# The gate and up products of both feed-forward layers: plain products over 512 tokens in place of Strassen's seven

## The chip, the cores and the metric

The kernel runs on one core of one Trainium2 chip. The metric is device time in microseconds (us) of one execution. Before the change it is 1904.37 us, the median of 3 runs (1902.75 to 1905.04). A TensorE instruction is called a product here: a stationary operand of 128x128 is loaded, and a moving operand of 256 or 512 columns is streamed through it into PSUM.

## The reference

Two layers act on 512 latent tokens and 256 context tokens, with 1024 features. Layer 0 mixes the tokens with a gated recurrence, layer 1 with windowed attention; each ends in a feed-forward part. Every half is wrapped in a norm that is scaled and shifted by vectors `ml`, `mc`, which come from products with `ada_w`. Only the latent tokens are returned. The part that the change touches is the first product of `swiglu`, `u @ w_in`, for the latent tokens of both layers:

```python
def swiglu(u, w_in, w_out):
    gt, up = jnp.split(u @ w_in, 2, axis=-1)
    return (jax.nn.silu(gt) * up) @ w_out
...
        x_lat = x_lat + ml[2] * rms_norm(y_lat, ng[1])
        h_lat = swiglu(modulate(x_lat, ng[2], ml[3], ml[4]), ffn_w_in[l], ffn_w_out[l])
        x_lat = x_lat + ml[5] * rms_norm(h_lat, ng[3])
```

`w_in` has 1024 rows and 2 x 2816 columns: 22 tiles of 128 gate features and 22 of up features.

## The kernel before

Activations lie feature-major: 8 tiles of 128 features x 512 tokens. Each fp32 operand is split into a high part (rounded to `fp32r`) and the rest, a low part, so that a product becomes three: high x high, low x high, high x low. The function `acc3` (line 180 issues it) does the three for each chunk of 128 contraction features. A weight tile of 128x1024 is loaded by SyncE (`raw`), cast on ScalarE or GpSimd (`whi`), and VectorE subtracts (`wlo`); `wload` does this for plain products (lines 130 to 133). There are four `raw`, three `whi` and three `wlo` buffers. `engines(ph)` names the engine of each stage's casts by a letter (`a` ScalarE, `p` GpSimd, `d` VectorE).

For the latent tokens a **unit** is one gate tile and one up tile. `ffn_in_s` does a unit by Strassen's method. `str_weights` loads the two tiles, forms sums and differences of quarters (lines 502 to 515, mostly on GpSimd, one on VectorE) and splits the seven results (`split`, lines 483 and 486). `str_unit` does seven products on quarters: 7 x 4 chunks x 3 = 84 products of 256 columns. It then combines the results on VectorE and ScalarE, and GpSimd multiplies by the gate (line 553). The moving operands `Uh`, `Ul`, and the sums of them that Strassen's products need, are made by `str_operand` (lines 568, 574 and 585 on VectorE), one half of the tokens after the other.

The rest of the program is written as generators. `merge(main, side, ratio)` gives the side `ratio` steps for each step of the main line, and a scheduler then orders all engines' instructions from that text, by priorities and a simulated timeline. Tiles of [128, 512] come from 63 slots, which a plan hands out by lifetimes; the `ar` tiles take such slots too. SyncE issues all transfers in one queue, in order.

The stages that matter, in order:
- "co": the context's output products (`ffn_out`), with the latent residual and `str_operand` beside them (`lat_mid`).
- Layer 0's feed-forward (`lat_ffn0`): 13 units, then the output products over these 13 hidden tiles (`out_part`), then 9 units. Beside it (`merge`, ratio 0.7) runs the context's residual and `ada_gen`, which makes layer 1's modulation vectors. `ada_gen` takes 80 tiles `ar` of 256 KB from memory and multiplies each (line 251) with a stationary operand of 32 columns, on one quarter of the array's columns: tile k goes to quarter k % 4. A Strassen unit is 8 steps of `merge`'s main line.
- "lo": the rest of the output products, and layer 1's norm of the context, which needs these vectors.
- Layer 1: attention, its output products ("wo", with 16 more `ar` tiles), and "f1": the first 5 units as plain products, 256 tokens at a time (`ffn_in_c`), the second half's residual and operands beside them. Then 8 Strassen units, output products, 9 Strassen units, and the last output products.

Of the kernel before, what the change touches and what calls it, by code (L numbers as in the profile page):

```python
# [45 lines left out]
def block_kernel(ctx, tc, plan, xT, cT, vecs, w2, cst, atm, rope, ada, rec_a, rec_v, rec_g, rec_o, qk_w, v_w, wo_w, ff_in, ff_out, out):  # L46
# [124 lines left out]
    def acc3(ps_, wparts, act):  # L171
        """three products a chunk; cfg["ll"]: those with the low part of the moving operand last."""
# [9 lines left out]
    def gemm_b(ps, whalves, ahi, alo, st, tt):  # L182
        """ps [128 tok, 256] = act[:, tok]^T w; whalves: (hi, lo) pieces of KD / len k x 256 columns."""
# [10 lines left out]
    # ---- PSUM: one bank per tile  # L194
# [13 lines left out]
    def follow(key, ins):  # L208
        """issue `ins` behind the last one of its lane on the same engine."""
# [8 lines left out]
    def psg():  # L218
        """accumulator of a dense product."""
# [4 lines left out]
    # ---- adaLN vectors, feature-major  # L224
# [45 lines left out]
    def scale_vec(a, g, plus_one, o=None, hfs=(0, 1)):  # L270
        """(1 + a) * g or a * g, both streams."""
# [9 lines left out]
    # ---- norms (feature-major)  # L281
    class Acc:
        """sums of squares over features, in two running parts [128, r, nt]; adds alternate
        between GpSimd and DVE where `dve` is set."""
# [9 lines left out]
        def add(self, src, sl, sv=None, own=False):  # L294
            """own: a tile of its own for these squares, which spares the addition."""
# [24 lines left out]
    def rstd_bc(acc, sl):  # L320
        """1 / rms of every token in sl, on all partitions (PSUM)."""
# [22 lines left out]
    def preload_sqrt():  # L344
        """brings the square root's table in behind what ACT has been given so far."""
# [12 lines left out]
    def norm_mod(tiles, acc, G, sh, j, u, sl, st=None):  # L358
        """u (hi, lo) = norm(x) * G + sh (acc None: tiles are normalised)."""
# [40 lines left out]
    def residual(tiles, ys, yacc, gg, j, xacc, sl, pat=""):  # L400
        """x += gate * norm(y); xacc collects the new x's squares."""
# [26 lines left out]
    def evac_y(st, m, p_, ys, yacc, sl):  # L428
        """projection output tile m: copy and squares."""
# [7 lines left out]
    def proj_out(st, src, nparts, a, ys, yacc, ms, sl):  # L437
        """feature-major output tiles ms of 128 features: src(m, part) -> (ap, n)."""
# [35 lines left out]
    # ---- Strassen's products for a dense layer on the latent tokens: two output tiles of features,  # L474
    # two halves of the contraction, two halves of the tokens.
    SCH = (("s2", "11", 0, 0), ("s5", "22", 0, 1), ("A22", "c", 1, 0), ("A11", "b", 1, 1), ("s1", "a", 3, 0), ("s7", "e", 2, 0),
           ("s6", "d", 2, 1))

    def split(src, w):
        hi = wp.tile([P, 1024], F32R, name=uid("whi"), tag="whi", bufs=WB)  # L480
        lo = wp.tile([P, 1024], F32R, name=uid("wlo"), tag="wlo", bufs=WB)
        if 'a' == "a":
            nc.scalar.copy(hi[:, :w], src)  # L483
        else:
            nc.gpsimd.tensor_scalar(hi[:, :w], src, 1.0, 0.0, ALU.mult, ALU.add)
        nc.vector.tensor_sub(lo[:, :w], src, hi[:, :w].bitcast(F32))  # L486
        return hi, lo

    def str_weights(src1, src2, w):
        """the seven stationary operands of [A11 | A12], [A21 | A22], w columns a quarter."""  # L490
        with tc.high_priority(offset=200):
            raw = []
            for s_ in (src1, src2):
                r = wp.tile([P, 1024], F32, name=uid("raw"), tag="raw", bufs=WB + 1)
                nc.sync.dma_start(out=r[:, : 2 * w], in_=s_)
                raw.append(r)
            g, u_ = raw
            L, R, B = slice(0, w), slice(w, 2 * w), slice(0, 2 * w)
            ws = hpool["p"].tile([P, 1024], F32, name=uid("ws"), tag="ws", bufs=WS)
            e = {"p": nc.gpsimd, "d": nc.vector}  # L500
            en = [e[c] for c in "pppdp"]
            en[0].tensor_sub(ws[:, R], u_[:, L], g[:, L])
            en[1].tensor_add(u_[:, L], u_[:, L], u_[:, R])
            en[2].tensor_add(ws[:, L], g[:, L], g[:, R])
            W = {}

            def put(hl, *names):
                for i, n_ in enumerate(names):
                    W[n_] = tuple(t[:, i * w : (i + 1) * w] for t in hl)

            put(split(u_[:, B], 2 * w), "s2", "A22")
            put(split(ws[:, B], 2 * w), "s5", "s6")
            en[3].tensor_sub(g[:, R], g[:, R], u_[:, R])  # L513
            put(split(g[:, B], 2 * w), "A11", "s7")
            en[4].tensor_add(g[:, L], g[:, L], u_[:, R])  # L515
            put(split(g[:, L], w), "s1")
        return W

    def str_unit(W, B, nk):
        """[C21 | C12] and [C11 | C22] in SBUF."""  # L520
        T = [None] * 4
        o = ut([P, 2, 256], name="so")
        x = ut([P, 2, 256], name="sx")
        y = ut([P, 2, 256], name="sy")
        for w, b, t, c in SCH:
            if T[t] is None:
                T[t] = ps("mm" if t == 3 else "kv").rearrange("p (c n) -> p c n", c=2)
            acc3(T[t][:, c, :], [W[w] + (nk,)], B[b])
            yield
            with tc.high_priority(offset=cfg["evp"]):  # L530
                if w == "s5":
                    nc.scalar.copy(y, T[0])
                elif w == "A11":
                    nc.vector.tensor_add(o, T[1], y)  # L534
                    for i in range(2):
                        nc.vector.tensor_sub(x[:, i, :], T[1][:, i, :], y[:, 1 - i, :])
                elif w == "s1":
                    m1 = ut([P, 256], name="m1")
                    nc.scalar.copy(m1, T[3][:, 0, :])
                elif w == "s6":  # L540
                    nc.vector.tensor_add(y, T[2], m1.unsqueeze(1).to_broadcast([P, 2, 256]))
        (nc.gpsimd if "p" == "p" else nc.vector).tensor_add(y, y, x)  # L542
        return o, y

    def ffn_in_s(l, U, h, ms, m0=0):
        for m in ms:
            W = str_weights(ff_in[l, m, 0], ff_in[l, m, 1], 512)
            o, y = yield from str_unit(W, U, 4)
            nc.scalar.activation(o[:, 1, :], o[:, 1, :], AF.Silu)
            nc.scalar.activation(y[:, 0, :], y[:, 0, :], AF.Silu)  # L550
            f = ut([P, 2, 256], name="fs")
            for i in range(2):
                (nc.gpsimd if "pp"[i] == "p" else nc.vector).tensor_mul(f[:, i, :], y[:, i, :], o[:, i, :])  # L553
            hh = h[0][m - m0]
            f = f.rearrange("p c n -> p (c n)").unsqueeze(1)
            nc.scalar.copy(hh, f)
            nc.vector.tensor_sub(h[1][m - m0], f, hh.bitcast(F32))
            yield

    def str_operand(tiles, xacc, G, sh, j, U, conv):  # L560
        """generators (one per token half) of the moving operands of u = norm(x) * G + sh; conv: also
        the plain parts of each half, for products without Strassen's sums."""
        F = [[None] * 4, [None] * 4]

# [12 lines left out]
        def half(hf):  # L577
# [21 lines left out]
            if hf == 0:  # L599
                return  # L600
# [1275 lines left out]
```

## Time and profile before

| what | value |
|---|---|
| median of 3 runs | 1904.37 us (1902.75 to 1905.04) |
| the profiled execution's own span | 1901.0 us |
| VectorE busy | 1277.6 us (67%) |
| ScalarE busy | 824.9 us (43%) |
| GpSimd busy | 875.7 us (46%) |
| mean granted TensorE clock | 0.969 |
| mean transfer rate | 121 GB/s |

The profile is of one execution; its times run from the start of its span. PE is TensorE, PEld its weight loads, DVE VectorE, ACT ScalarE, POOL GpSimd, SP SyncE. A name such as `ps_kv<-Uh,wlo` is output and inputs of an instruction, and L180 is the line that issued it. Products overlap in the pipeline, so the duration of one (0.28 us for 256 columns) says less than the step from one's start to the next one's.

### The profile page before, as it was taken

To read this page: it belongs to the slowest core of one execution; us is meant where nothing else is said; L and a number is where in the kernel's file an instruction comes from. 1 tells how busy PE (TensorE), PEld (TensorE's weight loads), DVE (VectorE), ACT (ScalarE), POOL (GpSimd) and SP (SyncE) were. 2 spreads that over 40 slices of the span, in tenths; PEclk is the share of its full clock that TensorE was granted. 3 is DMA by queue.
4 is the path that set the end of the run, shared out by engine and by line. 5 is a ranking of instruction groups with operands and counts; after the bars stand their busy time and mean duration, and the time that the engine had idled before them with its cause. 6 is when DMAs were issued, how large, how long until landed. Compare 5 with 4: busy or idle time off the path is not lost. (4 is left out here: it accounts for less than half of the span.)

```text
span 1901.0 us, 31663 instructions
## 1 busy us (share of the span) xinstructions
PE 1774.9 (93%) x12467; PEld 1537.4 (81%) x12467; DVE 1277.6 (67%) x1846; ACT 824.9 (43%) x1503; POOL 875.7 (46%) x789
## 2 busy tenths in 40 slices
PE   6889999998999999899999989899999888999897
PEld 3878678797999989776888888786787888888886
DVE  4985445566667529976853887778755988726866
ACT  3643554234645546443522443435755434403431
POOL 3665303334120026665632674424444657725755
PEclk9989999999999999899999999899999999999999
DMA  9435556210334544575232224311013432332233
GB/s 330 136 100 185 171 178 216 68 51 33 116 130 145 183 135 142 200 259 198 82 108 81 89 80 132 101 47 56 13 56 122 135 101 77 103 99 77 89 87 118
DMA packets 84005, 229.45 MB, mean 121 GB/s; under 512 B 9328, under 2 KB 14192, under 8 KB 83856
## 3 DMA queue, kind: packets, MB, share of 16 engines
q1 hardware_dynamic: 83856, 227.43, 37.0%
q8 instruction: 98, 1.61, 0.4%
q14 instruction: 51, 0.42, 0.1%
HBM read 225.30 MB, written 2.10 MB: 120 GB/s over the span
## 5 line engine op out<-in xcount | busy, mean ns | idle before, releaser
L133 DVE TENSOR_TENSOR wlo<-raw,whi 128x1024 fp32r<-128x1024 f32 x222 | 285.7, 1290 | 190.8 <-POOL whi L130 116.3
L180 PE MATMUL ps_kv<-Uh,wlo 128*128 128x256 f32 x1000 | 285.2, 293 | 40.6 <-DVE wlo L486 40.5
L130 POOL TENSOR_SCALAR whi<-raw 128x1024 fp32r<-128x1024 f32 (+2 forms) x153 | 172.2, 1128 | 251.3 <-PE ps_mm L180 81.9
L180 PE MATMUL ps_kv<-Uh,whi 128*128 128x256 f32 x1000 | 285.7, 291 | 0.0
L180 PE MATMUL ps_kv<-Ul,whi 128*128 128x256 f32 x1000 | 284.0, 289 | 0.0
L180 PEld LDWEIGHTS ps_kv<-Uh,wlo 128*128 128x128 f32 x1000 | 193.7, 197 | 55.7 <-DVE wlo L486 50.7
L180 PEld LDWEIGHTS ps_kv<-Uh,whi 128*128 128x128 f32 x1000 | 195.9, 197 | 12.2 <-issue 5.9
L180 PEld LDWEIGHTS ps_kv<-Ul,whi 128*128 128x128 f32 x1000 | 196.2, 197 | 1.8 <-issue 1.7
L486 DVE TENSOR_TENSOR wlo<-raw,whi 128x1024 fp32r<-128x1024 f32 (+1 forms) x117 | 155.7, 1331 | 58.0 <-ACT whi L483 57.3
L318 POOL TENSOR_TENSOR acc<-acc,sq 128x256 f32<-128x256 f32 (+1 forms) x79 | 91.7, 1163 | 206.6 <-ACT sq L317 205.8
L180 PE MATMUL ps_mm<-uh,wlo 128*128 128x256 f32 (+1 forms) x552 | 179.3, 326 | 5.4 <-DVE wlo L133 5.4
L180 PE MATMUL ps_mm<-uh,whi 128*128 128x256 f32 (+1 forms) x552 | 182.1, 331 | 2.0 <-POOL whi L130 2.0
L180 PE MATMUL ps_mm<-ul,whi 128*128 128x256 f32 (+1 forms) x552 | 179.4, 326 | 0.0
L483 ACT CAST whi<-raw 128x1024 fp32r<-128x1024 f32 (+1 forms) x117 | 105.6, 902 | 95.8 <-POOL raw L515 59.9
L132 ACT CAST whi<-raw 128x1024 fp32r<-128x1024 f32 (+2 forms) x85 | 83.8, 987 | 105.0 <-issue 45.4
L180 PEld LDWEIGHTS ps_mm<-uh,whi 128*128 128x128 f32 x552 | 106.4, 193 | 15.3 <-POOL whi L130 3.3
L180 PEld LDWEIGHTS ps_mm<-uh,wlo 128*128 128x128 f32 x552 | 106.3, 193 | 13.9 <-DVE wlo L133 6.0
L180 PEld LDWEIGHTS ps_mm<-ul,whi 128*128 128x128 f32 x552 | 106.3, 193 | 7.7 <-issue 0.5
L191 PE MATMUL ps_mm<-wlo,uh 128*128 128x256 f32 x344 | 100.5, 293 | 8.4 <-DVE wlo L133 8.4
L190 PE MATMUL ps_mm<-whi,uh 128*128 128x256 f32 x344 | 102.2, 299 | 0.7 <-ACT gate L925 0.5
L180 PE MATMUL ps_kv<-hh,whi 128*128 128x512 f32 (+1 forms) x277 | 99.4, 360 | 1.0 <-POOL whi L130 1.0
L180 PE MATMUL ps_kv<-hh,wlo 128*128 128x512 f32 (+1 forms) x277 | 99.4, 360 | 0.7 <-DVE wlo L133 0.7
(376 smaller groups left out, 5071.5 us busy)
## 6 DMA issues: line engine op xcount, KB each, us to landing
raw<-in_ff_in_dram SPq DMA_DIRECT2D x140, 512.0 KB, 3.5
ar<-in_ada_dram SPq DMA_DIRECT2D x192, 256.0 KB, 4.3
raw<-in_ff_out_dram SPq DMA_DIRECT2D x52, 512.0 KB, 3.6
raw<-in_rec_a_dram SPq DMA_DIRECT2D x34, 512.0 KB, 4.4
raw<-in_rec_v_dram SPq DMA_DIRECT2D x16, 512.0 KB, 3.3
raw<-in_rec_g_dram SPq DMA_DIRECT2D x16, 512.0 KB, 3.3
raw<-in_rec_o_dram SPq DMA_DIRECT2D x16, 512.0 KB, 3.5
raw<-in_wo_w_dram SPq DMA_DIRECT2D x14, 512.0 KB, 3.3
```

What stands on the lines that cost most here:

```text
L130: nc.gpsimd.tensor_scalar(hi[:, :n], raw[:, :n], 1.0, 0.0, ALU.mult, ALU.add)
L132: nc.scalar.copy(hi[:, :n], raw[:, :n])
L133: (nc.gpsimd if cfg["lo"][q % len(cfg["lo"])] == "p" else nc.vector).tensor_sub(lo[:, :n], raw[:, :n], hi[:, :n].bitcast(F32))
L180: mm(ps_, a, b, start=(i == 0), stop=(i == len(q) - 1))
L190: mm(ps, ah, hi[:, s], start=(k == 0), stop=False)
L191: mm(ps, ah, lo[:, s], start=False, stop=False)
L318: (nc.vector if i else nc.gpsimd).tensor_add(d, d, q)
L483: nc.scalar.copy(hi[:, :w], src)
L486: nc.vector.tensor_sub(lo[:, :w], src, hi[:, :w].bitcast(F32))
```

## The change

The functions for Strassen's products (`split`, `str_weights`, `str_unit`, `ffn_in_s`, `str_operand`) and `ffn_in_c` go. `ffn_in`, which the context's feed-forward uses already, serves all latent units: a unit is now 2 tiles x 8 chunks x 3 = 48 products of 512 columns. The operand is made by `norm_mod` as 8 plain tiles of high and low parts. In "f1" the first 5 units stay products of 256 columns; the weights of two units are now kept for the second half of the tokens, before those of one. The ratios of `merge` stay at 0.7 and go from 1.1 to 2.2 in "f1", while a unit is 2 steps now. ScalarE casts all weights of "l0" and "f1".

```diff
-    def ffn_in(st, l, u, h, ms, sl, m0=0):
+    def ffn_in(st, l, u, h, ms, sl, m0=0, hold=None, keep=()):
...
-                hi, lo = wload(ff_in[l, m, q], 1024)
+                w = wparts(ff_in[l, m, q], 1024, (m, q), hold if (m, q) in keep else None)
                 p_ = psg()[:, :n]
-                gemm_a(p_, [(hi, lo, KD)], u[0], u[1], st, sl)
+                gemm_a(p_, w, u[0], u[1], st, sl)
...
-    def ffn_in_s(l, U, h, ms, m0=0):
-        for m in ms:
-            W = str_weights(ff_in[l, m, 0], ff_in[l, m, 1], 512)
-            o, y = yield from str_unit(W, U, 4)
...
-        cfg["hi"], cfg["lo"] = {'co': ['a', 'ddp'], 'rb': ['p', 'ddp'], 'ci': ['a', 'd'], 'kv': ['a', 'ddp'], 'wo': ['pa', 'd'], 'l0': ['pa', 'd'], 'lo2': ['p', 'dp'], 'kw': ['a', 'd']}.get(ph, ("p", "d"))
+        cfg["hi"], cfg["lo"] = {'co': ['a', 'ddp'], 'rb': ['p', 'ddp'], 'ci': ['a', 'd'], 'kv': ['a', 'ddp'], 'wo': ['pa', 'd'], 'l0': ['a', 'd'], 'f1': ['a', 'd'], 'lo2': ['p', 'dp'], 'kw': ['a', 'd']}.get(ph, ("p", "d"))
...
-        half = str_operand(xl, xla, G2, ada0[3], 0, U2, False)
-        yield from seq(half(0), half(1))
+        u2.extend(new_u(SL))
+        yield from norm_mod(xl, xla, G2, ada0[3], 0, u2, FL)
...
-        yield from ffn_in_s(0, U2, hl0, range(GA))
+        yield from ffn_in(SL, 0, u2, hl0, range(GA), FL)
         yield from out_part(0, hl0, 0, GA, yl2, yla2, range(KD), FL, True, False)
         hl0 = new_h(SL, HID - GA)
-        yield from ffn_in_s(0, U2, hl0, range(GA, HID), GA)
+        yield from ffn_in(SL, 0, u2, hl0, range(GA, HID), FL, GA)
...
-        yield from half4(h)
+        yield from norm_mod(xl, xla1, G2, ada1[3], 0, u4, HS[h])
...
-    kf = [tuple(v) for v in [[0, 0], [0, 1]]]
-    drain(merge(seq(ffn_in_c(1, U4, hl1, range(N0), 0, hold_f, kf), ffn_in_c(1, U4, hl1, range(N0), 1, hold_f, kf)),
-                lat_next2(1), 1.1))
+    kf = [(m, q) for m in range(2) for q in range(2)]
+    drain(merge(seq(ffn_in(SL, 1, u4, hl1, range(N0), HS[0], 0, hold_f, kf),
+                    ffn_in(SL, 1, u4, hl1, range(N0), HS[1], 0, hold_f, kf)), lat_next2(1), 2.2))
...
-    drain(ffn_in_s(1, U4, hl1, range(N0, GB)), out_part(1, hl1, 0, GB, yf, yfa, range(KD), FL, True, False))
+    drain(ffn_in(SL, 1, u4, hl1, range(N0, GB), FL), out_part(1, hl1, 0, GB, yf, yfa, range(KD), FL, True, False))
     hl2 = new_h(SL, HID - GB)
-    drain(ffn_in_s(1, U4, hl2, range(GB, HID), GB))
+    drain(ffn_in(SL, 1, u4, hl2, range(GB, HID), FL, GB))
```

What the scheduler makes of it, at three places. First TensorE in layer 0's first units. Before, a visit to `ada_gen`'s products (L251) between Strassen's products takes up to 8 tiles `ar` in a row; here it takes 6:

```order
L180 MATMUL ps_kv_8386<-Ul_7652,whi_8327 128x256
L251 MATMUL ps_o_8366<-ar_8402,s_75 32x512
L251 MATMUL ps_o_8366<-ar_8417,s_75 32x512
L251 MATMUL ps_o_8366<-ar_8420,s_75 32x512
L251 MATMUL ps_o_8366<-ar_8439,s_75 32x512
L251 MATMUL ps_o_8366<-ar_8442,s_75 32x512
L251 MATMUL ps_o_8366<-ar_8472,s_75 32x512
L180 MATMUL ps_kv_8348<-Uh_7551,wlo_8328 128x256
```

In the changed program the first visit on TensorE takes 2 tiles between plain products of 512 columns:

```order
L180 MATMUL ps_mm_8387<-ul_7549,whi_8383 128x512
L180 MATMUL ps_mm_8387<-uh_7541,wlo_8384 128x512
L251 MATMUL ps_o_8417<-ar_8418,s_75 32x512
L251 MATMUL ps_o_8417<-ar_8421,s_75 32x512
L180 MATMUL ps_kv_8430<-uh_7534,whi_8426 128x512
```

The same 80 tiles stood in 27 visits, all within the first 13 units; they now stand in 45 (32 of two tiles, 12 of one, one of four), spread over both groups of units, the output products between them and the start of "lo".

Second, VectorE in "co", where the latent operand is made. Before (F is the normed tile, Ul the low part of an operand, Us a sum of two F), for the second half of the tokens:

```order
L585 SCALAR_TENSOR_TENSOR F_7884<-xl_7304,gv_3260,ps_tr_7773 128x256
...
L574 TENSOR_TENSOR Us_7988<-F_7546,F_7870 128x512
L574 TENSOR_TENSOR Us_7994<-F_7644,F_7870 128x512
L568 TENSOR_TENSOR Ul_8003<-Us_8000,Uh_8002 128x512
L568 TENSOR_TENSOR Ul_7876<-F_7870,Uh_7875 128x512
L568 TENSOR_TENSOR Ul_7896<-Us_7893,Uh_7895 128x512
```

Now (nt is the normed tile, ul its low part, wlo a weight's low part for the context's output products):

```order
L382 SCALAR_TENSOR_TENSOR nt_7664<-xl_7294,gv_3260,ps_tr_7563 128x512
L373 SCALAR_TENSOR_TENSOR ul_7543<-nt_7660,ada_1930,uh_7535 128x512
L382 SCALAR_TENSOR_TENSOR nt_7668<-xl_7296,gv_3260,ps_tr_7563 128x512
L133 TENSOR_TENSOR wlo_7786<-raw_7783,whi_7785 128x1024
L373 SCALAR_TENSOR_TENSOR ul_7544<-nt_7664,ada_1930,uh_7536 128x512
```

16 F, 14 Ul and 4 Us for the whole operand became 8 nt and 8 ul, with the weights' low parts between them.

Third, SyncE's queue at the end of layer 0's last 9 units in the changed program. The first of these `ar` tiles wait for products of the last unit to free their slots, and the weights of the output products (`in_ff_out`) stand behind them:

```order
L124 DMA raw_10421<-in_ff_out_dram 128x128
L248 DMA ar_10235<-in_ada_dram 128x512
L248 DMA ar_10238<-in_ada_dram 128x512
...
L248 DMA ar_10268<-in_ada_dram 128x512
L248 DMA ar_10271<-in_ada_dram 128x512
L124 DMA raw_10466<-in_ff_out_dram 128x1024
L248 DMA ar_10274<-in_ada_dram 128x512
L124 DMA raw_10472<-in_ff_out_dram 128x128
```

13 tiles `ar` stand in a row there; before, all 80 were loaded by the end of the first 13 units.

More of the change, by code (lines that the diff above doesn't have):

```diff
@@ L471, in ffn_in @@
             nc.vector.tensor_sub(ch(h[1], st, m - m0)[:, sl], s, hh.bitcast(F32))
-            yield
[L476 to L543, printed above, removed]
@@ L545, in ffn_in_s @@
-    def ffn_in_s(l, U, h, ms, m0=0):
-        for m in ms:
-            W = str_weights(ff_in[l, m, 0], ff_in[l, m, 1], 512)
-            o, y = yield from str_unit(W, U, 4)
[L549 to L558, printed above, removed]
@@ L560, in str_operand @@
-    def str_operand(tiles, xacc, G, sh, j, U, conv):
-        F = [[None] * 4, [None] * 4]
-        def hl(c, i, src):
-            hi, lo = (ht([P, 2, 256], name="U" + n_) for n_ in "hl")
-            nc.scalar.copy(hi, src)
-            nc.vector.tensor_sub(lo, src, hi.bitcast(F32))
-            for r in range(2):
-                U[c][2 * i + r] = (hi[:, r, :], lo[:, r, :])
-        def comb(c, i, a, b, sub, eng):
-            t = ut([P, 2, 256], name="Us")
-            (eng.tensor_sub if sub else eng.tensor_add)(t, a, b)
-            hl(c, i, t)
-        def half(hf):
-            sl = HS[hf]
-            bc = rstd_bc(xacc, sl)
-            yield
-            for i in (0, 2, 1, 3):
-                t = F[hf][i] = ut([P, 2, 256], name="F")
-                for r in range(2):
-                    k = 2 * i + r
-                    nc.vector.scalar_tensor_tensor(t[:, r, :], tiles[k][:, 0, sl], G[:, j, k : k + 1], bc[:, 0, :],
-                                                   ALU.mult, ALU.mult)
-                    ts_ = 'a'
-                    if ts_ == "a":
-                        nc.scalar.activation(t[:, r, :], t[:, r, :], AF.Identity, bias=sh[:, j, k : k + 1])
-                    else:
-                        nc.vector.tensor_scalar(t[:, r, :], t[:, r, :], sh[:, j, k : k + 1], None, ALU.add)
-                c = f"{i // 2 + 1}{hf + 1}"
-                if c in ("11", "22") or conv:
-                    hl(c, i % 2, t)
-                yield
-                if hf == 0 and i > 1:
-                    comb("c", i - 2, F[0][i], F[0][i - 2], True, nc.gpsimd)
-                    yield
-            if hf == 0:
-                return
-            cn = 'pddp'
-            e = {"p": nc.gpsimd, "d": nc.vector}
-            for i in range(2):
-                (b11, b21), (b12, b22) = ((F[h_][i], F[h_][i + 2]) for h_ in range(2))
-                for q, (c, x, y, sub) in enumerate((("b", b12, b22, True), ("a", b11, b22, False), ("e", b21, b22, False),
-                                                    ("d", b11, b12, False))):
-                    comb(c, i, x, y, sub, e[cn[q]])
-                    yield
-        return half
@@ L612, in new_U @@
-    def new_U():
-        return {c: [None] * 4 for c in ("11", "12", "21", "22", "a", "b", "c", "d", "e")}
-    def conv_u(U, hf):
-        return [U[f"1{hf + 1}"][k] for k in range(4)] + [U[f"2{hf + 1}"][k] for k in range(4)]
-    def gemm_c(ps_, parts, uc_):
-        acc3(ps_, parts, uc_)
-    def ffn_in_c(l, U, h, ms, hf, hold, keep):
-        sl = HS[hf]
-        for m in ms:
-            pg = []
-            for q in range(2):
-                p_ = psg()[:, :256]
-                gemm_c(p_, wparts(ff_in[l, m, q], 1024, (m, q), hold if (m, q) in keep else None), conv_u(U, hf))
-                pg.append(p_)
-                yield
-            s_ = ut([P, 256], name="fs")
-            with tc.high_priority(offset=cfg["evp"]):
-                nc.scalar.activation(s_, pg[0], AF.Silu)
-                nc.vector.tensor_mul(s_, s_, pg[1])
-            hh = h[0][m][:, 0, sl]
-            nc.scalar.copy(hh, s_)
-            nc.vector.tensor_sub(h[1][m][:, 0, sl], s_, hh.bitcast(F32))
@@ L1365, in block_kernel @@
     yc2, ya2 = new_ys(SC), Acc(SC)
-    U2 = new_U()
+    u2 = []
     xl = None
@@ L1644, in wo @@
             yield
-    U4 = new_U()
+    u4 = []
     gg1 = scale_vec(ada1[2], ng(1, 1), False)
     G2 = scale_vec(ada1[4], ng(1, 2), True)
-    half4 = str_operand(xl, xla1, G2, ada1[3], 0, U4, True)
     def lat_next2(h):
         yield from residual(xl, yw, ywa, gg1, 0, xla1, HS[h], {'ln1': 'pppppppp', 'lw1': 'dpdpdpdp', 'lw0': 'pdddpddd', 'la0': 'dpdpdpdd', 'la1': 'dpdpdpdd', 'ln0': 'dddpdddp', 'cm': 'pdddpddd', 'lm': 'dddpdddp'}.get("lw%d" % h, ""))
-        yield from half4(h)
+        if not u4:
+            u4.extend(new_u(SL))
+        yield from norm_mod(xl, xla1, G2, ada1[3], 0, u4, HS[h])
     drain(merge(piped([(b, kv) for kv in range(4) for b in (2, 3)], AD), wo(0), 0.09))
```

## The prediction

> **What bounds the kernel now.** I read the page first (TensorE busy 93% of the span), then the busy time of each engine by stage, then the waits of TensorE, then the timeline for the step from product to product. In the view by stage the columns are the stretch, its length, and busy time and instructions of PE, PEld, DVE, ACT, POOL, then granted clock, DMA share and GB/s:
>
> ```profile
> 505.00:660.00 155.00, 155.00 (x1381) 146.06 (x1381) 102.01 (x165) 79.45 (x146) 16.12 (x15) 1.00 0.48 156
> 742.00:783.00 41.00, 34.02 (x254) 33.61 (x253) 40.00 (x44) 26.13 (x48) 26.79 (x16) 0.88 0.51 159
> 783.00:971.00 188.00, 179.58 (x1290) 144.56 (x1289) 140.63 (x159) 79.39 (x125) 117.14 (x87) 0.99 0.53 176
> 971.00:1041.00 70.00, 70.00 (x311) 57.95 (x310) 25.68 (x21) 12.58 (x20) 19.41 (x16) 1.00 0.35 104
> 1041.00:1149.00 108.00, 97.33 (x762) 95.03 (x761) 85.83 (x86) 49.59 (x78) 75.75 (x57) 0.97 0.26 80
> 1556.00:1657.00 101.00, 88.33 (x676) 85.98 (x676) 80.28 (x79) 43.47 (x69) 67.97 (x51) 0.95 0.27 81
> 1727.00:1835.00 108.00, 97.04 (x759) 94.58 (x758) 82.92 (x82) 49.18 (x77) 73.23 (x55) 0.97 0.26 80
> ```
>
> The stretches are: the context's feed-forward, the second half of "co", layer 0's 13 units, output products, 9 units, then layer 1's 8 and 9 units. The last two stretches of plain products that need no Strassen sums (505 to 660, and 971 to 1041 with 512 columns) show TensorE busy without a gap. The four stretches of Strassen units do not: there VectorE is busy 75 to 79% of the time, and TensorE waits for it.
>
> ```profile
> PE ps_kv L180 <- DVE wlo L486: 40.5, 33, 3.0
> ```
>
> 33 waits for the low part of a Strassen weight make 40.5 us. So these stretches have two limits at once: TensorE's own steps, and a chain of GpSimd sums, casts and VectorE splits that comes late.
>
> **The steps.** Two rows each, first and last of a run without a gap, give the step of a product:
>
> ```profile
> 785.04 0.28 PE L180 MATMUL ps_kv<-Ul,whi 128*128 128x256 f32 x1
> ...
> 788.87 0.28 PE L180 MATMUL ps_kv<-Uh,wlo 128*128 128x256 f32 x1
> ...
> 1009.67 0.39 PE L180 MATMUL ps_kv<-hh,whi 128*128 128x512 f32 x1
> ...
> 1031.43 0.39 PE L180 MATMUL ps_kv<-hh,whi 128*128 128x512 f32 x1
> ```
>
> 32 steps in 3.83 us are 0.1197 us for 256 columns; 96 steps in 21.76 us are 0.2267 us for 512. The Trainium skill (TensorE: Matmul & The Clock Gate, Back-to-back issue gap) gives N/2.4 + 2.5 ns for an isolated step, and says that streams of weight loads and products sustain about 131 ns at 512 columns. The rows agree with neither: both shapes take some 11 ns more than the first, and 227 is far over 131.
>
> **1. Products.** A unit of 84 x 0.1197 = 10.05 us becomes 48 x 0.2267 = 10.88 us. There are 39 such units (22 + 17): **+32.2 us**. Strassen's seven products save an eighth of the columns, but twice as many instructions pay a fixed part each.
>
> **2. What Strassen's units lose to waits.** Their stretches, from first product to the first one behind:
>
> ```profile
> 1041.63 0.28 PE L180 MATMUL ps_kv<-Uh,whi 128*128 128x256 f32 x1
> ...
> 1148.72 0.40 PE L180 MATMUL ps_mm<-hh,whi 128*128 128x512 f32 x1
> ...
> 1556.17 0.28 PE L180 MATMUL ps_kv<-Uh,whi 128*128 128x256 f32 x1
> ...
> 1656.89 0.40 PE L180 MATMUL ps_kv<-hh,whi 128*128 128x512 f32 x1
> ...
> 1727.64 0.28 PE L180 MATMUL ps_kv<-Uh,whi 128*128 128x256 f32 x1
> ...
> 1835.23 0.40 PE L180 MATMUL ps_mm<-hh,whi 128*128 128x512 f32 x1
> ```
>
> Layer 0's 9 units took 107.1 us where 756 x 0.1197 = 90.5 would do: 16.6 lost. Layer 1: 100.7 less 672 x 0.1197 = 80.4, so 20.3, and 107.6 less 90.5, so 17.1. These hold the waits and, behind each long one, a stretch at half clock (0.95 to 0.97 granted). Layer 0's 13 units: 188.0 less 1092 x 0.1197 = 130.7, less 37.9 for the modulation products (point 3) and some 2 for small ones: 17.4. In all 71.4 us.
>
> What would wait in the plain units? Per unit VectorE then has two weights, a multiplication from PSUM and a low part, rows of which (mean ns) are:
>
> ```profile
> L133 DVE TENSOR_TENSOR wlo<-raw,whi 128x1024 fp32r<-128x1024 f32 x181 | 249.6, 1380 | 130.5 <-POOL whi L130 78.2 <-ACT whi L132 51.1 <-PE ps_mm L180 0.9
> L557 DVE TENSOR_TENSOR hl<-fs,hh 128x512 fp32r<-128x512 f32 x39 | 36.9, 947 | 16.4 <-ACT hh L556 16.1
> L534 DVE TENSOR_TENSOR so<-ps_kv,sy 128x512 f32<-128x512 f32 x39 | 26.9, 689 | 34.3 <-PE ps_kv L180 21.4 <-ACT sy L532 10.3 <-ACT sy L550 1.6
> ```
>
> 2 x 1.38 + 0.69 + 0.95 = 4.4 of 10.88 us, against 85.8 / 9 = 9.5 before, and GpSimd's 75.75 / 9 = 8.4 us fall to nothing. The context's feed-forward (505 to 660) runs the same code with the same engines at 256 columns, so with half the time for each weight, and TensorE was busy 155.00 of 155.00 us. Bounds: 0 and 71.4 remain; nearest to these rows is almost nothing. I leave 2: **-69.4 us**.
>
> **3. The modulation products (L251).** They stand in 45 visits instead of 27. What a visit costs:
>
> ```profile
> 783.51 0.28 PE L180 MATMUL ps_kv<-Ul,whi 128*128 128x256 f32 x1
> 783.72 1.04 PE L251 MATMUL ps_o<-ar,s 128*32 128x512 f32 x2
> ...
> 784.92 0.28 PE L180 MATMUL ps_kv<-Uh,whi 128*128 128x256 f32 x1
> ...
> 797.03 0.28 PE L180 MATMUL ps_kv<-Ul,whi 128*128 128x256 f32 x1
> 797.24 1.91 PE L251 MATMUL ps_o<-ar,s 128*32 128x512 f32 x12
> ...
> 799.30 0.28 PE L180 MATMUL ps_kv<-Uh,whi 128*128 128x256 f32 x1
> ```
>
> A tile shows as two records. One tile: 1.41 us less two ordinary steps = 1.17. Six tiles: 2.27 - 0.24 = 2.03. So up to four tiles, on the four quarters, go side by side in one pass of 0.86 us, and a visit adds 0.31. The 27 visits of before sum up to 27 x 1.18 + 7 further passes x 0.86 = 37.9 us, the 45 of after (none over four tiles) to 45 x 1.18 = 53.1: +15.2. In "wo" 16 tiles went in 3 visits of 2.03 and now go in one of 12 (2.9) and 4 of one: 7.6 for 6.1. Together **+16.7 us**. The Trainium skill (TensorEngine Tiling (Array Packing), Key Properties) speaks against the change here: a switch of the tiling mode drains TensorE. The 0.31 us agree with that; by the drains alone 18 more visits would be 18 x 0.31 = 5.6 us, the rest is passes with idle quarters.
>
> **4. "co".** In the 41.0 us of 742 to 783 TensorE did 240 products (28.7) and 14 small ones (1.4): 10.9 lost, to two waits and the half clock behind them:
>
> ```profile
> PE ps_mm L180 <- DVE wlo L133: 4.9, 1, 4.9
> PE ps_mm L180 <- POOL wlo L133: 2.1, 1, 2.1
> ```
>
> VectorE was busy 40.0 of these 41.0 us; weights stood behind the operand's sums:
>
> ```profile
> L568 DVE TENSOR_TENSOR Ul<-Us,Uh 128x512 fp32r<-128x512 f32 x10 | 13.7, 1383 | 0.0
> L585 DVE SCALAR_TENSOR_TENSOR F<-xl,gv,ps_tr 128x256 f32<-128x256 f32 x16 | 6.5, 473 | 0.7 <-PE ps_tr L341 0.7
> L419 DVE SCALAR_TENSOR_TENSOR xl<-y,gv,xl 128x512 f32<-128x512 f32 x6 | 7.4, 1241 | 0.1
> ```
>
> Now 16 operations like the last row (it is from the 35 us ahead) take at most 16 x 1.24 = 19.9 us and the weights some 9: 29 of 30. Bounds 0 and 10.9 lost; I leave 1.5: **-9.4 us**.
>
> **5. "f1".**
>
> ```profile
> 1482.15 0.39 PE L180 MATMUL ps_mm<-Uh,whi 128*128 128x256 f32 x1
> ...
> PE ps_mm L180 <- DVE wlo L133: 6.0, 3, 3.0
> PE ps_mm L180 <- DVE Ul L568: 1.7, 2, 1.5
> ```
>
> From here to 1556.17 are 74.0 us for 480 products (57.5) and 14 small ones (1.4): 15.1 lost. The products stay; VectorE's queue loses the sums, but two more kept weights are split in it just ahead of the first half's last chunks, and the second half's chunks are due a few products after their norm. So waits will move, not all go. Bounds 0 and 15.1; I leave 6: **-9.1 us**.
>
> **6. "lo".** The last 14 tiles `ar` are loaded only when the last unit frees their slots, and their products stand one by one among the output products. TensorE's own work there is 14 x 1.18 us and 30 products of 0.2267, more than 23 us, while 3.7 MB at the 176 GB/s of the 13 units are 21 us. So the loads nearly keep pace. The context's norm comes later, but 36 us of products still cover it. Nothing to 10 us; I take **+3**.
>
> **Sum**: 32.2 - 69.4 + 16.7 - 9.4 - 9.1 + 3 = -36.0 us, against the profiled execution (span 1901.0, 3.4 below the median, as start and end lie outside it). Predicted: 1904.4 - 36.0 = 1868.4 us.
>
> **Rivals.** *The waits in "co" and "f1" come back in another form*, since VectorE must still make operand and weights in one queue: points 4 and 5 give 0, and the time is 1868 + 18.5 = 1887. For it: every wait there is VectorE's, which stays full. Against it: its work in "co" falls from 40.0 us to some 29. 14%.
>
> *The plain units wait for each weight* (ends slower). The cast now stands on ScalarE behind Silu and the cast of h, which wait for TensorE; VectorE's part stands behind both. 78 weights at the mean of the 33 old waits (1.23 us) cost 96 us: 1965. From 0.46 us a weight on the gain of 36 is gone. Against it stand the gapless 155 us of the same code. 3%. Likewise, 45 visits that each wait for their tile as the worst did before (1.3) would add 58, giving 1927; before, only 2 of 27 waited. 2%.
>
> ```profile
> PE ps_o L251 <- DMA ar<-in_ada_dram: 1.9, 2, 1.3
> ```
>
> *512 columns cost less in a dense stream.* At 131 ns a unit would take 6.3 us: 39 x 4.6 = 179 us less, 1690. That is the page's sustained figure; 96 steps at 227 exclude it. Under 1%. *The change doesn't reach the chip's order* is excluded: the changed program has no Strassen operand, and 3585 products of 512 columns at line 180, where 1713 stood.
>
> **How the numbers follow.** 80% for the forecast, whose own range is 1854 to 1884 (points 2, 4, 5, 6 at their likelier ends: -14, +16). The first rival reaches 1890. The range 1853 to 1890 leaves out the slower cases and the tails. Runs of this kernel differ by about 0.1%, so 0.2% (3.8 us) is what can be told from no change: faster 0.93, same 0.02, slower 0.05.
>
> **What would show it.** TensorE in the four stretches of plain units: one product each 0.2267 us, near 98 us for each 9 units, no row of waits for `wlo` over 2 us in all. Layer 0 from the first unit to the end of "lo" (404 us before) hardly shorter: the gain of points 1 and 2 (-16 there) is eaten by point 3; the gain shows in "co" and layer 1. L251: 45 visits. Wrong would be: waits of TensorE for casts on ScalarE, or for `ar` at the start of "lo", or "f1" as long as before.

## The result, and the profile after

The changed kernel takes 1855.88 us (median of 4 runs, 1854.45 to 1859.08) against 1903.56 us for the kernel before on the same chip: a ratio of 0.9759, 95% interval 0.9744 to 0.9774, so 47.7 us less where 36.0 were predicted. The profiled executions give 1854.5 against 1901.0 us, 46.5 less.

The view by stage of the changed kernel, in the columns used above (stretch, length, busy time of PE, PEld, DVE, ACT, POOL, granted clock, DMA share, GB/s); the rows are the second half of "co", layer 0's 13 units, the output products, the 9 units but for their last 6 us, these with most of "lo", "f1", layer 1's 8 units and its 9 units:

```profile
743.00:773.00 30.00, 29.39 (x242) 28.92 (x242) 23.79 (x24) 17.56 (x25) 11.48 (x6) 1.00 0.62 185
773.00:932.00 159.00, 159.00 (x694) 119.70 (x692) 55.91 (x67) 48.33 (x63) 3.29 (x2) 1.00 0.46 147
932.00:1009.00 77.00, 77.00 (x334) 59.07 (x334) 17.37 (x17) 17.53 (x24) 0.00 (x0) 1.00 0.41 125
1009.00:1116.00 107.00, 107.00 (x458) 77.39 (x457) 31.44 (x34) 26.13 (x34) 1.35 (x2) 1.00 0.39 124
1116.00:1179.00 63.00, 63.00 (x254) 38.84 (x254) 29.93 (x62) 15.43 (x29) 13.96 (x15) 1.00 0.47 150
1470.00:1534.00 64.00, 63.95 (x508) 60.55 (x507) 43.43 (x78) 34.49 (x59) 6.36 (x7) 1.00 0.43 138
1534.00:1621.00 87.00, 87.00 (x387) 72.09 (x386) 28.99 (x32) 24.55 (x32) 0.00 (x0) 1.00 0.32 96
1692.00:1790.00 98.00, 98.00 (x434) 81.12 (x434) 31.44 (x34) 26.32 (x34) 1.35 (x2) 1.00 0.28 88
```

TensorE has no gap in any stretch of units, and the granted clock is 1.00 throughout. VectorE falls from 82.92 us to 31.44 in layer 1's 9 units, GpSimd from 73.23 to 1.35. First product of that stretch, and first product behind it, in the timeline of the changed kernel:

```profile
1692.06 0.39 PE L180 MATMUL ps_mm<-uh,whi 128*128 128x512 f32 x1
...
1789.98 0.39 PE L180 MATMUL ps_kv<-hh,whi 128*128 128x512 f32 x1
```

97.92 us for 9 x 48 = 432 products are 0.2267 us each, the step of before to the last digit.

TensorE's waits for `wlo` in the changed kernel (total, times, longest), over the whole run and then from 743 to 1192 us:

```profile
PE ps_mm L180 <- DVE wlo L133: 7.2, 6, 2.8
```

```profile
PE ps_mm L180 <- DVE wlo L133: 0.5, 1, 0.5
```

The row of 40.5 us for Strassen's weights has no successor: what is left lies nearly all ahead of the change.

The stages, from first product to first product in the traces (us). "Lead" is all up to "co"'s first output product; layer 0 is its 13 units, output products, 9 units and "lo"; "before again" is e10 below:

| kernel | lead | "co" | layer 0 | attention, "wo" | "f1" and 8 units | out | 9 units | last |
|---|---|---|---|---|---|---|---|---|
| before | 700.4 | 82.7 | 420.8 | 278.2 | 174.7 | 70.7 | 107.6 | 52.7 |
| before again | 699.9 | 82.5 | 418.3 | 277.4 | 174.2 | 70.7 | 107.0 | 52.3 |
| after | 701.4 | 72.0 | 418.6 | 277.7 | 151.7 | 70.7 | 97.9 | 50.8 |
| e2 no weight sums | 701.9 | 79.9 | 381.0 | 284.5 | 155.6 | 71.5 | 92.3 | 51.2 |
| e4 visits of four | 704.2 | 72.0 | 390.6 | 278.2 | 151.7 | 70.7 | 97.9 | 50.8 |
| e5 plain in layer 0 | 708.4 | 72.0 | 418.6 | 279.4 | 172.3 | 70.7 | 107.5 | 51.3 |
| e6 plain in layer 1 | 703.8 | 83.5 | 424.1 | 280.8 | 151.6 | 70.7 | 97.9 | 50.8 |
| e9 no GpSimd sums | 699.9 | 79.6 | 394.0 | 277.4 | 156.9 | 71.3 | 92.3 | 52.6 |

So the gain is 10.7 us in "co", 2.2 in layer 0, 23.1 in "f1" and the 8 units, 9.7 in the 9 units, 1.9 in the last outputs and 0.5 in the attention, less 1.0 in the lead. Layer 0 as a whole gave almost nothing, as predicted; the experiments say why.

### The profile page after: what moved, and what is told of

It is laid out like the page before. It is cut to its first block, busy times and chain, and to the rows that moved or that the text cites. A ratio compares the mean times of both kernels' runs of the same rounds, so it can differ in the third digit from the quotient of the medians.

```text
span 1854.5 us, 27784 instructions
## 1 busy us (share of the span) xinstructions
PE 1788.4 (96%) x11063; PEld 1469.8 (79%) x11063; DVE 981.7 (53%) x1587; ACT 747.1 (40%) x1313; POOL 434.2 (23%) x460
## 4 chain that ended last, share of the span: by engine, by line
PE 53%; DVE 5%; ACT 1%; issue 1%; POOL 0%; DVEq 0%; ACTq 0%
PE ps_kv L180 25%; PE ps_mm L180 20%; PE ps_o L251 3%; PE ps_o L1437 2%; PE ps_tr L1430 2%; DVE xl L419 1%; PE ps_kv L1396 1%; PE ps_kv L1397 1%; DVE P L1399 1%; DVE QS L1350 1%; DVE wlo L133 1%; ACT P L1412 1%; PE ps_tr L334 0%; DVE y L412 0%; PE ps_tr L341 0%
## 5 line engine op out<-in xcount | busy, mean ns | idle before, releaser
L133 DVE TENSOR_TENSOR wlo<-raw,whi 128x1024 fp32r<-128x1024 f32 (+3 forms) x296 | 365.2, 1236 | 410.9 <-ACT whi L132 319.7
L132 ACT CAST whi<-raw 128x1024 fp32r<-128x1024 f32 (+2 forms) x199 | 200.7, 1010 | 491.7 <-issue 187.4
L130 POOL TENSOR_SCALAR whi<-raw 128x1024 fp32r<-128x1024 f32 (+1 forms) x113 | 122.2, 1084 | 817.4 <-PE ps_mm L180 374.3
L180 PE MATMUL ps_mm<-ul,whi 128*128 128x512 f32 (+1 forms) x840 | 287.3, 342 | 0.0
L180 PE MATMUL ps_kv<-uh,whi 128*128 128x512 f32 (+1 forms) x696 | 247.8, 356 | 0.0
L180 PE MATMUL ps_kv<-uh,wlo 128*128 128x512 f32 (+1 forms) x696 | 244.9, 352 | 1.6 <-DVE wlo L133 1.5
L180 PE MATMUL ps_kv<-ul,whi 128*128 128x512 f32 (+1 forms) x696 | 244.8, 352 | 0.0
L180 PEld LDWEIGHTS ps_mm<-ul,whi 128*128 128x128 f32 x840 | 161.8, 193 | 16.7 <-issue 0.6
L180 PEld LDWEIGHTS ps_kv<-uh,whi 128*128 128x128 f32 x696 | 131.7, 189 | 34.9 <-ACT whi L132 11.7
L180 PEld LDWEIGHTS ps_kv<-uh,wlo 128*128 128x128 f32 x696 | 131.6, 189 | 19.6 <-DVE wlo L133 1.9
L180 PEld LDWEIGHTS ps_kv<-ul,whi 128*128 128x128 f32 x696 | 131.8, 189 | 16.7
```

Source lines behind the costliest of these rows:

```text
L130: nc.gpsimd.tensor_scalar(hi[:, :n], raw[:, :n], 1.0, 0.0, ALU.mult, ALU.add)
L132: nc.scalar.copy(hi[:, :n], raw[:, :n])
L133: (nc.gpsimd if cfg["lo"][q % len(cfg["lo"])] == "p" else nc.vector).tensor_sub(lo[:, :n], raw[:, :n], hi[:, :n].bitcast(F32))
L180: mm(ps_, a, b, start=(i == 0), stop=(i == len(q) - 1))
```

## The experiments

Ratios are to the kernel before, with 95% intervals.

**e1: every 512-column product of the plain units as two of 256.**

```diff
-                gemm_a(p_, w, u[0], u[1], st, sl)
+                for hs in (HS if n == 512 else (sl,)):
+                    gemm_a(p_[:, hs] if n == 512 else p_, w, u[0], u[1], st, hs)
```

> The changed kernel, but every product of 512 columns in the 39 plain units is issued as two of 256, so that a unit has 96 products of the short kind. Nothing else is touched. Theory (the price of a unit is its count of products times the step of its shape, as in point 1): 96 x 0.1197 = 11.49 us instead of 10.88, 39 x 0.61 = +23.8 us, so about 1880 us, with TensorE still busy without a gap. Rival (what is saved or lost goes by columns and weight chains only, and the short step costs nothing more): no change, 1856 us.

1881.79 us, 0.9883 (0.9863 to 0.9904): 25.9 us above the changed kernel, where 23.8 were expected. The view by stage for its 8 units of layer 1 has

```profile
1548.00:1640.00 92.00, 92.00 (x769) 92.00 (x769) 28.98 (x32) 24.39 (x32) 0.00 (x0) 1.00 0.28 92
```

92 us for 768 products are 0.1198 each, so point 1's price is right: 384 more products over the same columns cost some 5 us, 13 ns each. What these 13 ns are is not shown. PEld is busy 92.00 of 92 us here and 72.09 of 87 in the same stage after, but that doesn't make the weight loads the limit. The record of a load (second figure behind the bar, in ns) is as long here as after:

```profile
L180 PEld LDWEIGHTS ps_kv<-uh,whi 128*128 128x128 f32 x144 | 27.7, 192 | 0.0
```

```profile
L180 PEld LDWEIGHTS ps_kv<-ul,whi 128*128 128x128 f32 x72 | 13.5, 188 | 2.8
```

Here a load starts every 0.12 us, so that the records overlap each other and fill the time whatever the limit is.

**e2: Strassen without its weight sums.**

```diff
-            en[0].tensor_sub(ws[:, R], u_[:, L], g[:, L])
-            en[1].tensor_add(u_[:, L], u_[:, L], u_[:, R])
-            en[2].tensor_add(ws[:, L], g[:, L], g[:, R])
+            ws = g
...
-            en[3].tensor_sub(g[:, R], g[:, R], u_[:, R])
-            en[4].tensor_add(g[:, L], g[:, L], u_[:, R])
```

> The kernel before, with the five sums a unit left out that make Strassen's weights (four on GpSimd, one on VectorE); the casts, low parts, products and sums behind the products stay, so the result is not the reference's. Theory (the 71.4 us that Strassen's units lost are the late chain of sums, casts and low parts, and the half clock behind each wait): the units run at 84 x 0.1197 = 10.05 us; layer 0's 9 units near 91 us, layer 1's 8 and 9 near 81 and 91, the 13 units lose almost nothing; the modulation products also stand in 16 visits of 23 passes instead of 27 of 34 in layer 0, 13 us less. About 1904 - 71 - 13 = 1820 us, less than the changed kernel. Rival (the loss lies elsewhere, in VectorE's sums behind the products or in the PSUM banks): hardly more than the 13 us, 1890.

1830.37 us, 0.9608 (0.9584 to 0.9632). Both 9-unit stretches took 92.3 us, or 1.8 above 756 x 0.1197, in place of 107.1 and 107.6. In all 73.3 us were gained where 84 were expected; 6.3 of the difference is a longer attention and "wo", which this edit doesn't touch; why they were longer stays open. The theory of point 2 holds: without the sums Strassen's units are faster than the plain ones, at 92.3 against 97.9. The plain products win because they need no sums, not because they are cheaper.

**e9: only GpSimd's four sums left out; VectorE's stays.** It is as e2, with this line kept on VectorE:

```diff
+            nc.vector.tensor_sub(g[:, R], g[:, R], u_[:, R])
```

> The kernel before, with the four sums a unit on GpSimd left out that make Strassen's weights; the fifth, on VectorE, stays, so VectorE has all the work it had. The result is not the reference's. Theory (the waits come from the hop over GpSimd ahead of the casts, and from what it does to VectorE's durations, not from VectorE's share of busy time): the 9 units take 92 to 94 us as without any sums (92.3), with VectorE busier there than the 76% of that run; about 1838 us. Rival (VectorE's load is the limit, and the run without sums went faster as it took a sum from VectorE): the 9 units take 98 us or more, 1860 or more.

1835.16 us, 0.9641 (0.9625 to 0.9657), with 92.8 and 92.3 us for the two stretches of 9 units: what the units lost goes with GpSimd's four sums. The expectation was wrong in one thing: VectorE isn't busier than in e2 but less, 67.01 of 93 us, since its durations fell. Groups by shape in the 9 units of layer 0, VectorE's split of `raw` (mean ns of one), first before, then e2, then e9:

```profile
L486 DVE TENSOR_TENSOR wlo<-raw,whi 128x1024 fp32r<-128x1024 f32 x17 | 25.9, 1521 | 6.6 <-ACT whi L483 6.5
```

```profile
L486 DVE TENSOR_TENSOR wlo<-raw,whi 128x1024 fp32r<-128x1024 f32 x25 | 37.6, 1529 | 9.2 <-ACT whi L483 9.2
```

```profile
L486 DVE TENSOR_TENSOR wlo<-raw,whi 128x1024 fp32r<-128x1024 f32 x25 | 30.4, 1236 | 13.8 <-ACT whi L483 13.8
```

e2's splits of `raw` are as slow as before's, 1.53 us, and still no product waits for one, so the pace of these splits was not the whole cause. Before's splits of GpSimd's sums (`ws`) and VectorE's own sum (L513) were slower still, where that sum (L508 in e9) took 0.68 us without GpSimd's; first before, then e9:

```profile
L486 DVE TENSOR_TENSOR wlo<-ws,whi 128x1024 fp32r<-128x1024 f32 x8 | 15.2, 1904 | 0.0
L513 DVE TENSOR_TENSOR raw<-raw,raw 128x512 f32<-128x512 f32 x7 | 12.5, 1780 | 0.2 <-DMA raw<-in_ff_in_dram 0.2
```

```profile
L508 DVE TENSOR_TENSOR raw<-raw,raw 128x512 f32<-128x512 f32 x8 | 5.5, 681 | 0.0
```

What a unit's last weights wait for stands in before's rows for their cast and for the sum ahead of it:

```profile
L483 ACT CAST whi<-raw 128x512 fp32r<-128x512 f32 x9 | 5.6, 621 | 17.9 <-POOL raw L515 17.1 <-PE ps_kv L180 0.8
```

```profile
L515 POOL TENSOR_TENSOR raw<-raw,raw 128x512 f32<-128x512 f32 x9 | 11.6, 1292 | 17.6 <-DVE wlo L486 17.6
```

ScalarE stood idle 17.1 us for GpSimd's last sum (L515), and GpSimd 17.6 us for VectorE's split (L486), which must have read the tile that the sum overwrites. By the code a unit's last weights so ran through a sum on VectorE, a cast on ScalarE, a split on VectorE, a sum on GpSimd, a cast and a split, one behind the other. In e2 and e9 that last cast waits 2.0 and 0.8 us, and for TensorE alone. No run keeps GpSimd's sums and has VectorE as fast as in e9, so it stays open how much of the loss was the hop itself and how much VectorE's slower work beside it.

**e3: Strassen without the operand's sums.**

```diff
-            t = ut([P, 2, 256], name="Us")
-            (eng.tensor_sub if sub else eng.tensor_add)(t, a, b)
-            hl(c, i, t)
+            for r in range(2):
+                U[c][2 * i + r] = U["11"][2 * i + r]
```

> The kernel before, with the five sums of the moving operand and their casts and low parts left out in both layers (the plain part of one quarter stands in for each), so the result is not the reference's; the weights' sums stay. Theory (points 4 and 5: the waits at the end of co and in f1 are these sums ahead of the weights in VectorE's queue): co from 40.7 to about 30.5 us, f1 from 74.0 to about 65, while the four stretches of Strassen units lose as much as before (107, 101 and 108 us). The modulation products stand in 16 visits of 27 passes, 10 us less. About 1904 - 10 - 9 - 10 = 1875 us. Rival (the weights alone fill VectorE there): co and f1 keep 5 us or more of their loss each, about 1885.

1882.63 us, 0.9892 (0.9867 to 0.9918), between the two. The waits of "co" are nearly gone, as the theory has it: 0.6 us in its second half, where 7.0 stood before; the view by stage has TensorE busy 39.70 of 40 us at the full clock:

```profile
743.00:783.00 40.00, 39.70 (x310) 34.72 (x310) 25.69 (x34) 23.00 (x44) 18.00 (x13) 1.00 0.79 267
```

"co" is only 4.7 us shorter all the same, since modulation products moved into it (x310 where x254 stood): four visits, 6.4 us by the prices of point 3. "f1" and the 8 units fell by 10.3 us, 9.6 of them in "f1", as expected. In layer 0 the waits for Strassen's weights grew instead, from 17.0 to 24.1 us; the row is of the whole run:

```profile
PE ps_kv L180 <- DVE wlo L486: 47.5, 29, 4.5
```

That is 7.0 us more than the 40.5 of before, all of it in layer 0. The weights' waits don't go with the operand's sums: they have a cause of their own.

**e4 and e8: visits of four.** Modulation products are issued for four quarters together, with 1.1 side steps per main step; e4 everywhere, e8 only beside layer 0's feed-forward.

```diff
-            for q in range(4):
+            for q2 in range(2):
...
-drain(merge(lat_ffn0(), side, 0.7))
+drain(merge(lat_ffn0(), side, 1.1))
```

> The changed kernel, but the modulation products are written four at a time, for the four quarters, with 1.1 side steps per main step instead of 0.7: 20 visits of exactly four tiles in layer 0 instead of 45, and none among lo's output products. Theory (a visit costs 0.31 us and a pass 0.86, whatever of the four quarters it uses): 25 x 1.18 = 29.5 us less, and 1.6 less in lo, so about 1826 us. Rival 1 (a visit now waits for the last of four loads, at the 1.3 us that the worst waited before): 20 x 1.3 = 26 us of it go again, 1852. Rival 2 (only the switch costs, passes lie beside the products): 25 x 0.31 = 8, 1848.

1831.07 us, 0.9617 (0.9601 to 0.9634), 24.8 us below the changed kernel. Layer 0 is 28.0 us shorter; the lead is 2.8 longer. A visit of four tiles (two records a tile) in e4, then one of two tiles in the changed kernel:

```profile
822.14 0.39 PE L180 MATMUL ps_mm<-uh,wlo 128*128 128x512 f32 x1
822.45 1.07 PE L256 MATMUL ps_o<-ar,s 128*32 128x512 f32 x8
823.45 0.50 PE L180 MATMUL ps_mm<-uh,whi 128*128 128x512 f32 x1
823.79 0.39 PE L180 MATMUL ps_mm<-ul,whi 128*128 128x512 f32 x1
```

```profile
835.69 0.39 PE L180 MATMUL ps_kv<-uh,wlo 128*128 128x512 f32 x1
836.01 1.05 PE L251 MATMUL ps_o<-ar,s 128*32 128x512 f32 x4
836.99 0.50 PE L180 MATMUL ps_kv<-uh,whi 128*128 128x512 f32 x1
837.33 0.39 PE L180 MATMUL ps_kv<-ul,whi 128*128 128x512 f32 x1
```

From the product ahead to the second one behind are 1.65 and 1.64 us; less two steps of 0.2267, a visit costs 1.20 and 1.19. Four tiles cost what two do. At the 0.31 us of the switch alone 25 visits fewer would have saved 8 us, not 28: the pass is what is paid. The Trainium skill (TensorEngine Tiling (Array Packing), Key Properties) says only that a switch of the tiling mode drains TensorE, which by these rows is the smaller part.

> As the run with visits of four tiles, but only for layer 1's vectors, whose products stand beside layer 0's units; the modulation products of layer 0 ahead of them, which in that run made the part up to co 2.7 us longer, are as in the changed kernel. Theory: the part up to co as in the changed kernel, layer 0 from its first unit on 28 us shorter, about 1828 us, below both kernels. Rival (the 2.7 us are not from those visits but another order of everything): 1831 again.

1830.67 us, 0.9618 (0.9600 to 0.9635): the rival. The lead is 704.4 us here too, though nothing in it was edited. All of the difference lies in one place; the view by stage, first after, then e8:

```profile
340.00:355.00 15.00, 14.88 (x79) 10.13 (x78) 10.36 (x29) 7.21 (x11) 3.78 (x3) 1.00 0.28 92
```

```profile
340.00:355.00 15.00, 14.88 (x52) 9.49 (x51) 10.42 (x28) 7.05 (x12) 3.77 (x3) 0.77 0.26 87
```

The granted clock is 0.77 over 15 us, which costs 15 x 0.23 = 3.5 us. e4 has the same stretch, so its longer lead was not the edit's doing either.

**e5 and e6: the change in one layer alone** (the other as before).

> The change in layer 0 alone; layer 1 is that of the kernel before. Theory (the stages' gains add up, and layer 0's is small since the 45 visits of the modulation products and the dearer products eat what the waits gave): co 40.7 to 30, first unit to the end of lo 404 to 405, lo's second half 3.6 less; in all about -12, 1891 us. Rival (layer 0's waits set how layer 1 starts, or the gain is one of the whole kernel, so half of it shows in each layer): -24, 1880.

> The change in layer 1 alone; layer 0 is that of the kernel before, with its modulation products in 24 visits of 29 passes instead of 27 of 34, which is 5 us less. Theory: f1 and the 8 units 174.7 to about 152, the 9 units 107.6 to 98, the rest 2 to 3 less; with the 5 us some -40, 1864 us. Rival (half of the gain in each layer): -24 - 5, 1874.

1895.76 us, 0.9962 (0.9949 to 0.9974), and 1875.92 us, 0.9853 (0.9832 to 0.9873). By the totals both theories look wrong: 8 and 28 us don't make 48. The table shows why. Each layer's own stages repeat the changed kernel: e5 has 72.0 and 418.6 us in "co" and layer 0; e6 has 151.6, 97.9 and 50.8 in layer 1. In e5 the lead is 8.0 us longer than before, and in e6 3.4 us longer, with 3.3 more in its layer 0 and 2.6 more in the attention, all in parts that the edits leave as they are. The modulation products' 5 us in e6 didn't come: in its layer 0 TensorE waited 24.6 us for Strassen's weights, where it had waited 17.0 before, and 3.5 us for `ar` tiles, where it had waited 1.9.

**e10 and e11: one more profile of before and of e5.**

> The kernel before once more, one profile. In ten kernels the part up to the first output product of co, which none of them but one edits, took from 700.4 to 708.4 us. Theory (that is a property of each kernel, from the slots that its tiles are planned into anew and the order that follows): 700 to 701 again, and every stage within 1 us of the first profile. Rival (it differs from execution to execution): anywhere from 699 to 708.

> The run with the change in layer 0 alone once more, one profile. Theory (property of the kernel): the part up to co 708 again, 8 us more than before, span 1894. Rival (of the execution): nearer to 703, span near 1889.

Before again: lead 699.9 us, its time 1897.69 us in that single run. e5 again: lead 706.7, time 1892.88, with a span of 1891.1 where 1894 was expected. So the lead is largely each kernel's own (700 against 707 to 708), and not an execution's; "lo" alone differed by 2.2 us between the two executions of before (55.2 and 53.0), and the other stages by less than 1.

Part of the lead is the clock. The stretch of e8 near 348 us, 6.8 us at half clock, stands in the traces of e1 to e6, e8 and e11 and in none of the others. In all, the clock was at half for 41.0 us of before's lead and 37.5 of its repeat's, for 47.8 of e5's and 44.4 of its repeat's. If such time counts half, the lead is 680 to 682 us in every run but e5 and its repeat, which have 684.5 both (an estimate from the granted clock in the traces). So of e5's 8.0 us some 3.4 are clock and 4.5 its own, and what e4 and e8 have more than the changed kernel is all clock.

**e7: casts on the engines of before.**

```diff
-'l0': ['a', 'd'], 'f1': ['a', 'd'],
+'l0': ['pa', 'd'],
```

> The changed kernel with the casting engines of before: every second weight of layer 0's units, and all weights of f1 and of layer 1's units, are cast on GpSimd instead of ScalarE. Theory (with plain weights the chain is short enough on either engine): the four stretches of units stay within 1 us of 158, 107, 87 and 98, only f1, where VectorE is fullest, grows by up to 4: 1856 to 1860 us. Rival (the move of the casts to ScalarE carries much of the gain): waits for wlo in every stretch, 1870 or more.

1856.26 us, 0.9749 (0.9732 to 0.9767), the same as the changed kernel. "f1" took 70.4 us instead of 64.6, more than the 4 us longer that were expected, and two more modulation visits are 2.4 of it; the attention and "wo" ahead of it were 5.3 us shorter, as these visits and some of the work left them. The stretches of units didn't move: 87.1 and 97.9 us in layer 1. The casts' move to ScalarE carries none of the whole gain.

**e12: two kept weights in "f1" instead of four.**

```diff
-kf = [(m, q) for m in range(2) for q in range(2)]
+kf = [(0, 0), (0, 1)]
```

> The changed kernel with the two kept weights of before in f1 instead of four; the other two are loaded and split again for the second half. Theory of point 5 (the splits of the two more kept weights stand ahead of the first half's last chunks and make part of f1's loss): f1 up to 2 us shorter than 64.6. Rival (f1 loses only some 2 us in all, to the first chunk of the operand, and the kept weights are not in its way): f1 within 1 us of 64.6, the whole within 3 us of 1856.

1862.82 us, 0.9786 (0.9770 to 0.9803): 6.9 us slower than the changed kernel. Both expectations missed. "f1" took 70.7 us instead of 64.6 (two more modulation visits of one tile among it), and TensorE's waits there, absent in the changed kernel, are

```profile
PE ps_o L251 <- DMA ar<-in_ada_dram: 1.3, 2, 0.8
PE ps_mm L180 <- ACT uh L389: 1.1, 1, 1.1
PE ps_mm L180 <- DVE ul L373: 0.9, 1, 0.9
PE ps_tr L341 <- DVE rs L338: 0.6, 1, 0.6
```

The first row belongs to the two visits that moved in. The waits for `rs`, `uh` and `ul`, 2.6 us, stand at 1507 to 1511 us, where the second half of the tokens begins and two weights more are to be split: its norm comes late there.

## Why the prediction was right, and where it was off

1. **Products, +32.2.** Right. The stretches of plain units took 87.07 us for 384 products and 97.92 for 432, both 0.2267 each, and e1 put the price back from the other side. (84 products against 48 are 1.75 times as many, not twice.)

2. **Waits of Strassen's units, -69.4.** Right in mechanism, and the 2 us left were nothing: the 8 and the 9 units of layer 1 have no loss at all. By e2 and e9 the loss came from GpSimd's sums, and by before's rows from the last of them, a hop in a chain of six steps; it was not VectorE's share of busy time (76% in e2 without such a wait, 80% before with 16.6 us lost). Whether the sums also cost by slowing VectorE down is not separated. The prediction named "a chain of GpSimd sums, casts and VectorE splits", which was right; that VectorE was busy 75 to 79% of the time was no evidence for it.

3. **Modulation products, +16.7.** Right. Measured visits cost 1.19 instead of 1.18, and e4 took 28.0 us out of layer 0 by 25 fewer of them (1.12 each, with "lo"'s small gain in it). They are why layer 0 gave 2.2 us where layer 1 gave 35, and why layer 0's 9 units took 113.6 us and not the 98 that the prediction named for each 9: 13 visits stand among them, and without these it is 98.1. In "wo" the visit of 12 tiles took 3.9 us, where three passes, 2.9, were costed.

4. **"co", -9.4.** Right. Its second half went from 40.7 to 30.3 us and the whole by 10.7; the 1.5 us left were 0.6 (29.39 busy of 30). VectorE was busy 23.79 of 30 us there, less than the 29 that were allowed at most. e3 shows that the operand's sums made the waits.

5. **"f1", -9.1.** This is the term that was mis-sized. From 74.0 us it fell to 64.6, and those hold three modulation visits, 3 x 1.18 = 3.5 us, booked under point 3. Products 57.5, small ones 1.4, visits 3.5 leave 2.2 lost, where 6 were left: less the visits, 12.9 us were gained where 9.1 were forecast. The wrong step was "two more kept weights are split in it just ahead of the first half's last chunks": e12 shows the opposite sign. Kept weights spare VectorE their second split exactly when the second half's norm is due. With two instead of four "f1" is 6.1 us longer: 2.4 us are two more visits, 1.3 the waits for these visits' tiles, and 2.6 the waits for the norm and its operands.

6. **"lo", +3.** Nothing. TensorE is busy 63.00 of 63.00 us from 1116 on, and no wait for `ar` shows; only the visits of point 3 are paid. Its second half, not in the sum, gained 3.6 us. The repeated profile of before differs by 2.2 us in "lo", so part of that is an execution's own.

The sum missed by 10.5 us of span: 3.8 in "f1", 3.6 in "lo"'s second half, 1.9 in the last outputs, some 3 in units and "lo", 1.3 in "co", less some 3 by which the lead, the attention with "wo" and the end of the span came out longer than the sum has them. All but those of "lo"'s second half and the last outputs are allowances for waits that did not come. The 5.5 us of these two are in no term of the sum, and in part luck: e5, whose layer 1 is that of before, has the last outputs at 51.3 us where before has 52.7. The prediction costed the work well and was too careful with the leftovers, so that the time lies 2 us above the lower end, 1854, of the forecast's own range. None of its rivals came about: no wait per weight, none per visit, and none in "co" or "f1" in another form.

## What to carry to other kernels

A scheme that saves products by making more operands is paid in the chain that makes them: look at how many engines a weight crosses, and take the sums away once to see what it costs (here 34 us in layer 1's 17 units, where the products saved 14). Small products squeezed between large ones are paid by the visit: pack the four quarters before issuing, which gave another 25 us, so that the version of e8 (1830.67 us) beats both kernels. And compare stages, not totals, where a plan is made anew for each version: stages that no edit touched moved by up to 8 us, about 3.4 of them time at half clock, so that the granted clock belongs in the comparison.

## What the runs showed of the hardware

At full clock a product costs 0.1197 us at 256 columns and 0.2267 at 512, each with its own weights. The second 256 columns of a product cost 0.107 us, so about 0.013 us of each product don't depend on its columns, if columns cost the same in both; e1 measures the same 13 ns.

Short waits cost the clock as well. In layer 1's 9 units of before the longest wait was 2.1 us, and yet the clock granted there was 0.97 on average:

```profile
PE ps_kv L180 <- DVE wlo L486: 10.9, 9, 2.1
```

10.9 us of waits and 0.03 x 107 = 3.2 us of clock make 14.1 of the 17.1 lost; the rest stays open. Behind two of the nine waits, one of 1.8 and one of 2.1 us, the clock was at half for 3.4 us; behind two others of 2.0 us it was not. The view by stage from 1756.7 us on, just behind the first:

```profile
1756.70:1760.10 3.40, 3.40 (x18) 3.40 (x18) 1.65 (x3) 1.45 (x3) 3.32 (x4) 0.50 0.37 122
```

The Trainium skill (TensorE: Matmul & The Clock Gate, HAM oscillation — how this bites in real kernels) puts the rule at gaps of more than about 3.4 us. Here gaps of 2.1 us and less were enough, and in e8 a stretch at 0.77 appeared with no wait in the list at all. What set it off in e8 and not in the changed kernel stays open.
